# A hybrid attention layer: the order of loads, fillers and small operations ahead of its first projection

## The chip, the cores and the metric

The kernel runs on one core of a Trainium2 chip. The metric is device time in microseconds of one execution; the median of several runs counts. Five engines work side by side, each through its own queue in order: PE (matmuls; its loads of weights are shown as PEld), DVE (VectorE), ACT (ScalarE), POOL (GpSimd) and SP, which here issues DMAs only. They wait for one another and for DMAs by semaphores.

## The reference, cut to what matters

One decoder layer: a modulated norm, one projection, two groups of attention heads, an output projection with a gate. The change touches only the first two lines and the gate's factor.

```python
mod = jax.nn.silu(c) @ w_ada + b_ada
shift, scale, gate = jnp.split(mod, 3, axis=-1)
h = rms_norm(x, norm_gain) * (1 + scale[:, None, :]) + shift[:, None, :]
proj = h @ w_in
...                      # sliding-window heads, compressed/selected/window heads, z gates
out = y.astype(x.dtype) @ w_out
return x + gate[:, None, :] * out
```

x is 512 x 1024 in f32, c has 1024 values, `w_ada` is 1024 x 3072, `w_in` 1024 x 3096.

## The kernel before, in words

x is held transposed: eight tiles `xT[k]` of 128 channels x 512 tokens. Everything is f32, and most products are split in a high and a low part (`hh`, `hl` of h; `wh`, `wl` or `swh`, `swl` of a weight), so that a product is three matmuls.

Phase one makes h and the first projection (`first_proj`, L286 and L287: 768 columns into six PSUM banks) channel tile by channel tile. For a tile k it needs the root of the mean square of x for all 512 tokens (so all eight tiles of x), and the tile's shift and scale.

*The head* is all that stands ahead of tile 0. In the order of the code: SP issues x's tiles 0 to 2, the constants `first` (c in columns, `b_ada`, `norm_gain`, an identity) and `bias`, x's tiles 3 to 7, and then for four tiles the modulation weights (`ada`, two DMAs of 512 KB) and the first projection's weights (`wst`, 384 KB), then `rest`. PE runs 16 filler matmuls on zeros (`dummies`, L310). ACT squares each tile of x (L325) and DVE adds the squares of four tiles (L327); PE sums them over the channels with a column of ones (L339), after tile 3 and after tile 7. silu(c) is made in columns as c(1+tanh(c/2))/2 (L323, L329, L330). Between the last squares PE spreads it along a row with eight transposes (L333); ACT copies that row to all partitions as `scrow` (L342). PE then multiplies the bias table by its one-hot matrix (L335), and ACT copies the result (L343, L344), which two DMAs store to DRAM for the attention biases.

After L339's second group DVE makes the root (L351, then eight operations of `rsqrt`, L101 to L108). PE modulates tile 0 (`mod_pe`, L230: 8 products of 32 columns against `ada[0]`), ACT copies the result (`macc`, L233), PE sums it over partitions (`mod_col`, L250) and spreads the root with four transposes (L357), followed by three fillers. DVE finishes shift and scale (`mod_ab`, L255 and L256, columns of `AB`) and multiplies x by the root (`scaled`, L270), ACT applies shift and scale (`hh`, L365), and the first projection starts.

Tile 1 is modulated by PE in the same way, in the middle of tile 0's projection; `PE_MODS = 2` says so. For the other six tiles DVE does it with two long multiply-and-sum operations over 1024 columns each (`mod_rows`, L222), which read `scrow`. `new_tile(k)` queues, in this order, ACT's `hh` and `hf` of tile k, DVE's `mod_rows(k+1)`, `hl` of tile k (L279), `scaled(k+1)`, and the split of the next `wst` (`swh` on ACT, L262; `swl` on DVE, L265).

`in_order(tc)` around phase one keeps every engine's instructions in the order in which the code writes them. Which tiles share storage is found by the allocator, and a shared place adds waits that the code doesn't show. The later phases (other projections in a stream beside the attention slots, then the output projection) are unchanged but for `gate_slice` (L686), which reads `scrow` too.

Of the kernel before, what the change touches and what calls it, by code (L numbers as in the profile page):

```python
# [29 lines left out]
WAIT_L, WAIT_M = 4, (0, 8)  # L30
PER_A, PER_B = 3.6, (3.5, 1.6, 7)
NEAR = 256
ND = (16, 0, 3)
NR = 4
LW = 4
PE_MODS = 2
# [45 lines left out]
def hybrid_layer_kernel(ctx, tc, A, out):  # L82
# [14 lines left out]
    def rsqrt(v, n):  # L97

        y = sm.tile([128, n], F32, name="n_y")
        t = sm.tile([128, n], F32, name="n_t")  # L100
        DVE.tensor_scalar(y.bitcast(I32), v.bitcast(I32), -0.5, float(MAGIC), op0=OP.mult, op1=OP.add)  # L101
        DVE.tensor_tensor(t, y, y, op=OP.mult)
        DVE.scalar_tensor_tensor(t, t, -0.375 * NEWTON[0], v, op0=OP.mult, op1=OP.mult)
        DVE.scalar_tensor_tensor(y, t, 0.375 * NEWTON[0] * NEWTON[1], y, op0=OP.add, op1=OP.mult)
        DVE.tensor_tensor(t, y, y, op=OP.mult)
        DVE.scalar_tensor_tensor(t, t, 64.0 / 9.0, v, op0=OP.mult, op1=OP.mult)
        DVE.scalar_tensor_tensor(t, t, -10.0 / 3.0, t, op0=OP.add, op1=OP.mult)
        DVE.scalar_tensor_tensor(y, t, 5.0, y, op0=OP.add, op1=OP.mult)  # L108
        return y
# [20 lines left out]
    nsink = con.tile([128, 8], F32, name="nsink")  # L130
    sc_col = con.tile([128, 8], F32, name="sc_col")
    prm1 = con.tile([128, 8], F32, name="prm1")
    prmg = con.tile([128, 8], F32, name="prmg")
    va = con.tile([128, NB, 128], F32, name="va")
    vs = con.tile([128, NB, 128], F32, name="vs")
    vw = con.tile([128, NB, 128], F32, name="vw")
# [74 lines left out]
    def load_wst(k):  # L211
        wst[k] = wst_ring[:, k % NR]
        SP.dma_start(wst[k], A["w_qkv_a"][k])
# [4 lines left out]

    def mod_rows(k):

        for e, (factor, start) in enumerate(((1.0, prm[:, k:k + 1]), (prm[:, 24 + k:25 + k], prmg[:, k:k + 1]))):
            DVE.tensor_tensor_reduce(out=ada[k][:, e], in0=ada[k][:, e], in1=scrow, scale=factor, scalar=start,  # L222
                                     op0=OP.mult, op1=OP.add, accum_out=AB[:, k, 1 - e:2 - e])

# [39 lines left out]
    def weights_low(k):  # L264
        DVE.tensor_tensor(ws[k][1], wst[k], ws[k][0].bitcast(F32), op=OP.subtract)  # L265
# [24 lines left out]
    with in_order(tc) as begun:  # L290
        zero = con.tile([128, 512], BF16, name="zero")
        DVE.memset(zero, 0.0)
        DVE.memset(ada_ring[:, 0, 0:1], 0.0)
        DVE.memset(wst_ring[:, 0, 0:1], 0.0)
        POOL.memset(lsb[0:8, 0:LINE - NEAR], BIG)
        for k in range(8):
            SP.dma_start(xT[k], A["xT"][k])
            if k == 2:
                SP.dma_start(first, A["first"])
                SP.dma_start(bl, A["bias"])  # L300
        for k in range(NR):
            load_ada(k)
            load_wst(k)
        SP.dma_start(rest, A["rest"])
        DVE.memset(scz, 0.0)


        def dummies(n):
            for _ in range(n):
                PE.matmul(pj_kv[0].rearrange("p a b -> p (a b)"), zero[:, 0:128], zero, start=True, stop=True)  # L310

        dummies(ND[0])

        halves = [slice(0, 256), slice(256, 512)]
        pr = ps_pj.tile([128, 512], F32, name="pj")
        pl = pj_q[1][0:40, 0:NEAR]
        th = con.tile([128, 8], F32, name="th")
        for k in range(8):
            sq = stp.tile([128, S], F32, name="sacc") if k == 4 else T2(F32, "sq")
            if k % 4 == 0:  # L320
                sacc = sq
            if k == 4:
                ACT.activation(th, cT, AF.Tanh, scale=0.5)  # L323
            for c in (halves if k == 7 else [slice(0, S)]):
                ACT.activation(sq[:, c], xT[k][:, c], AF.Square)  # L325
                if k % 4:
                    DVE.tensor_tensor(sacc[:, c], sacc[:, c], sq[:, c], op=OP.add)  # L327
            if k == 4:
                DVE.scalar_tensor_tensor(sc_col, th, 1.0, cT, op0=OP.add, op1=OP.mult)  # L329
                DVE.tensor_scalar(sc_col, sc_col, 0.5, None, op0=OP.mult)  # L330
            if k == 7:
                for j in range(8):
                    PE.transpose(pj_q[2 + j // 4][:, 128 * (j % 4):128 * (j % 4) + 128],  # L333
                                 sc_col[:, j:j + 1].to_broadcast([128, 128]), ident)
                PE.matmul(pl, bl[:, NEAR:NEAR + 40], bl[:, 0:NEAR], start=True, stop=True)  # L335
                dummies(ND[1])
            if k % 4 == 3:
                for tb in range(NB):
                    PE.matmul(pr[:, tb:tb + 1], sacc[:, tb * 128:(tb + 1) * 128], ones, start=k == 3 and tb == 0,  # L339
                              stop=k == 7 and tb == NB - 1, skip_group_check=True)  # L340
        for e in range(2):
            ACT.activation(scrow[:, 512 * e:512 * e + 512], pj_q[2 + e], AF.Copy)  # L342
        ACT.copy(lsb[0:40, LINE - NEAR:LINE], pl)  # L343
        ACT.copy(lsb[32:40, 0:LINE - NEAR], lsb[32:40, LINE - NEAR:LINE - NEAR + 1].to_broadcast([8, LINE - NEAR]))  # L344
        for a in range(2):
            SP.dma_start(line_d[a], lsb[32 * a:32 * a + 8, :])
        DVE.tensor_copy(scz[:, :, 0], sc_col)
        DVE.tensor_scalar(prm1, prm[:, 8:16], 1.0, None, op0=OP.add)
        DVE.tensor_tensor(prmg, prm1, prm[:, 24:32], op=OP.mult)
        sx = con.tile([128, NB], F32, name="sx")  # L350
        DVE.tensor_scalar(sx, pr[:, 0:NB], 1.0 / D, EPS, op0=OP.mult, op1=OP.add)  # L351
        rx = rsqrt(sx, NB)
        mod_pe(0)
        mod_col(0)
        rbp = ps_pj.tile([128, 512], F32, name="pj")
        for tb in range(NB):
            PE.transpose(rbp[:, tb * 128:(tb + 1) * 128], rx[:, tb:tb + 1].to_broadcast([128, 128]), ident)  # L357
        dummies(ND[2])
        weights_high(0)
        mod_ab(0)  # L360
        scaled(0, rbp, halves)
        rb = stp.tile([128, S], F32, name="rb")
        hf[0] = T2(F32, "hf")
        for c in halves:
            ACT.activation(hh[0][:, c], y[0][:, c], AF.Identity, bias=AB[:, 0, 1:2], scale=AB[:, 0, 0:1])  # L365
        ACT.activation(rb, rbp, AF.Copy)
        ACT.activation(hf[0], y[0], AF.Identity, bias=AB[:, 0, 1:2], scale=AB[:, 0, 0:1])
        weights_low(0)
        scaled(1, rb)
        h_low(0)  # L370
        weights_high(1)
        weights_low(1)

        def new_tile(k):

            h_high(k, halves if k < 4 else (slice(0, S),))
            if k < 7:
                mod_rows(k + 1)
            h_low(k)
            if k < 7:  # L380
                scaled(k + 1, rb)
                weights_high(k + 1)
                weights_low(k + 1)

        for k in range(8):
            if k + NR < 8:
                load_ada(k + NR)
                load_wst(k + NR)
            elif k == LW:
                for _ in range(5):  # L390
                    load_next()
            for n in range(3):
                first_proj(k, n)
                if k == 0 and n == 0:
                    mod_pe(1)
                if k < 7 and n == 1:
                    if k == 0:
                        mod_col(1)
                        mod_ab(1)
                    new_tile(k + 1)  # L400
                if k >= 6 and n == 1:
                    split_to("kv_cmp", 2 * (k - 6) + 1, 0)
        DVE.tensor_tensor(kg[:, 0], qga, kga, op=OP.mult)
        DVE.tensor_tensor(kg[:, 1], qgb, kgs, op=OP.mult)
        DVE.tensor_tensor(kg[:, 2], qgb, kgw, op=OP.mult)
        DVE.tensor_tensor(kg[:, 3], qgb, kgc, op=OP.mult)
        DVE.tensor_scalar(kg[:, 0:3], kg[:, 0:3], -(HD ** -0.5), None, op0=OP.mult)
        DVE.tensor_scalar(kg[:, 3], kg[:, 3], HD ** -0.5, None, op0=OP.mult)
        DVE.tensor_scalar(nsink, sinks, -1.0, None, op0=OP.mult)
# [272 lines left out]
    def gate_slice(q):  # L682

        for h in range(2):
            n, w = 2 * q + h, raws[f"gate{q}", h]
            DVE.tensor_tensor_reduce(out=w, in0=w, in1=scrow, scale=1.0, scalar=prm[:, 16 + n:17 + n],  # L686
                                     op0=OP.mult, op1=OP.add, accum_out=gate[:, n:n + 1])
            load_next()
            yield 0.0
# [327 lines left out]
def _layout(inp):  # L1017
# [47 lines left out]
    for n in range(2):  # L1065
        bias[0:32, NEAR + 32 * n:NEAR + 32 * n + 8] = g("rel_bias")[:, 8 * n:8 * n + 8]
        bias[32, NEAR + 32 * n:NEAR + 32 * n + 8] = 1.0
    a["bias"] = bias
    return a


# [14 lines left out]
```

## Time and profile before

| what | value |
|---|---|
| runs of the kernel | 320.7, 320.85 (median), 322.26 us |
| profiled execution, whole time | 322.89 us |
| profiled execution, span | 321.1 us |
| PE busy | 310.7 us (97% of the span) |
| DVE busy | 236.4 us (74%) |
| ACT busy | 196.2 us (61%) |
| mean granted clock of PE | 0.978 |

Times in views are microseconds from the start of the span. A line of the timeline has start, length, engine, source line, operation, the tile written and the tiles read, shape, count, and in brackets the idle time before it with what ended it. A line of the windows has a stretch, its length, busy time and count of each engine, the granted share of PE's clock, the DMA share and GB/s. The column of the clock shows 1.00 before its first recorded change, at 6.85 us; the first sixteen fillers start 0.43 us apart up to there, and matmuls of the same 512 columns later in the run 0.23 us apart.

### The profile page before, as it was taken

What the parts mean: (1) busy time and instruction counts of PE and PEld (TensorE: products, weight loads), DVE (VectorE), ACT (ScalarE), POOL (GpSimd) and SP (SyncE); (2) the same over time, 40 slices, a digit from 0 to 9 for tenths busy, and PEclk for the clock granted to TensorE, in tenths of its full rate; (3) what the DMA queues carried; (4) which work ended last, traced back from release to release, by engine and by line L of the source; (5) the groups of instructions that cost most, each with busy time, mean ns of one, the idle gap of its engine ahead of it and who ended that gap; (6) DMA issues with size and microseconds to landing.
All of it is one profiled execution on the core that took longest, in us unless ns stands there. A gap on an engine that the chain in (4) does not pass through costs nothing.

```text
span 321.1 us, 5773 instructions
## 1 busy us (share of the span) xinstructions
PE 310.7 (97%) x2093; PEld 254.2 (79%) x2094; DVE 236.4 (74%) x655; ACT 196.2 (61%) x472; POOL 3.8 (1%) x21
## 2 busy tenths in 40 slices
PE   7899999999999999999999999999999999999995
PEld 2658878879888899999875788878788878788883
DVE  2548999999996467898998899989776678544220
ACT  4646556948886667495946766878785877513000
POOL 0000000000000000000000000000000000000000
PEclk9659999999999999999999999999999999999999
DMA  6999946910084535461263202322320210153201
GB/s 223 387 408 407 395 144 182 331 42 0 9 276 146 174 123 154 143 219 45 61 233 134 66 2 67 131 65 68 114 83 2 67 65 3 63 168 95 101 33 65
DMA packets 27943, 44.11 MB, mean 137 GB/s; under 512 B 1755, under 2 KB 19324, under 8 KB 27916
## 3 DMA queue, kind: packets, MB, share of 16 engines
q1 hardware_dynamic: 26764, 41.66, 37.8%
q10 hardware_dynamic: 1152, 2.10, 2.2%
q8 instruction: 16, 0.26, 0.3%
q14 instruction: 11, 0.09, 0.1%
HBM read 41.61 MB, written 2.14 MB: 136 GB/s over the span
## 4 chain that ended last, share of the span: by engine, by line
PE 61%; DVE 24%; DMA 6%; ACT 4%; issue 3%; SPq 1%; DVEq 0%; ACTq 0%
PE pj L465 25%; PE po L926 7%; PE s L851 7%; PE pj L455 4%; PE pt L909 4%; DVE wl L174 4%; DMA raw<-in_w_gate 3%; DVE ada_ring L222 3%; PE pt L899 3%; PE s L584 2%; DVE qs L516 2%; DMA xTp<-in_xT 1%; DMA ada_ring<-in_w_ada_rows 1%; DVE pa L856 1%; PE po L932 1%
## 5 line engine op out<-in xcount | busy, mean ns | idle before, releaser
L173 ACT ACTIVATE wh<-raw 128x512 fp32r<-128x512 f32 (+1 forms) x52 | 31.2, 634 | 13.5 <-PE pj L465 13.3
L174 DVE TENSOR_TENSOR wl<-raw,wh 128x512 fp32r<-128x512 f32 (+1 forms) x52 | 34.6, 690 | 5.4 <-ACT wh L173 3.4
L455 PE MATMUL pj<-wl,hh 128*128 128x256 f32 (+1 forms) x128 | 36.8, 288 | 0.2
L455 PE MATMUL pj<-wh,hh 128*128 128x256 f32 (+1 forms) x128 | 36.8, 288 | 0.0
L455 PE MATMUL pj<-wh,hl 128*128 128x256 f32 (+1 forms) x128 | 36.4, 284 | 0.0
L863 ACT ACTIVATE pp<-pp,nm 128x256 f32<-128x256 f32 (+2 forms) x48 | 29.3, 613 | 6.8 <-DVE nm L856 6.6
L465 PE MATMUL pj<-hh,wh 128*128 128x512 f32 x80 | 32.2, 402 | 0.0
L465 PE MATMUL pj<-hh,wl 128*128 128x512 f32 x80 | 31.9, 398 | 0.0
L465 PE MATMUL pj<-hl,wh 128*128 128x512 f32 x80 | 31.8, 398 | 0.0
L856 DVE CUSTOM_DVE_ANT_0 pp<-s,bias 128x256 f32<-128x256 f32 (+2 forms) x48 | 25.5, 552 | 3.7 <-PE s L851 3.5
L465 PE MATMUL pj<-yl,wh 128*128 128x512 f32 x64 | 25.2, 397 | 0.0
L465 PE MATMUL pj<-yh,wh 128*128 128x512 f32 x64 | 25.2, 397 | 0.0
L465 PE MATMUL pj<-yh,wl 128*128 128x512 f32 x64 | 25.0, 394 | 0.0
L1013 DVE SCALAR_TENSOR_TENSOR fin<-pj,gate,xr 128x512 f32<-128x512 f32 x8 | 6.0, 751 | 25.4 <-PE pj L465 25.4
L455 PEld LDWEIGHTS pj<-wl,hh 128*128 128x128 f32 x128 | 24.1, 188 | 0.7 <-DVE wl L174 0.7
L455 PEld LDWEIGHTS pj<-wh,hh 128*128 128x128 f32 x128 | 24.0, 188 | 0.3 <-issue 0.2
L455 PEld LDWEIGHTS pj<-wh,hl 128*128 128x128 f32 x128 | 24.1, 189 | 0.2 <-issue 0.2
L851 PE MATMUL s<-kTb,qs 128*128 128x256 f32 (+2 forms) x96 | 23.5, 356 | 0.0
L884 DVE TENSOR_SCALAR pp<-pp,rr,grev 128x256 f32<-128x256 f32 (+2 forms) x48 | 21.1, 477 | 0.7
L910 ACT COPY ptT<-pt 128x384 f32<-128x384 f32 (+1 forms) x32 | 15.8, 531 | 7.2 <-PE pt L909 6.8
L900 ACT COPY ptT<-pt 128x512 f32<-128x512 f32 (+1 forms) x28 | 15.5, 553 | 6.7 <-PE pt L899 6.5
L465 PEld LDWEIGHTS pj<-hh,wh 128*128 128x128 f32 x80 | 15.0, 188 | 3.8 <-issue 1.2
(233 smaller groups left out, 710.7 us busy)
## 6 DMA issues: line engine op xcount, KB each, us to landing
ada_ring<-in_w_ada_rows SPq DMA_DIRECT2D x12, 512.0 KB, 8.1
raw<-in_w_cmp SPq DMA_DIRECT2D x8, 512.0 KB, 7.7
raw<-in_w_gate SPq DMA_DIRECT2D x8, 512.0 KB, 5.3
raw<-in_w_o SPq DMA_DIRECT2D x8, 512.0 KB, 3.8
wst_ring<-in_w_qkv_a SPq DMA_DIRECT2D x8, 384.0 KB, 7.8
xTp<-in_xT SPq DMA_DIRECT2D x8, 256.0 KB, 4.7
ada_ring<-in_w_ada_cols SPq DMA_DIRECT2D x4, 512.0 KB, 7.9
bias<-line_d SPq DMA_DIRECT2D x8, 256.0 KB, 3.1
```

Of the source, the lines that this page charges most:

```text
L173: ACT.activation(wh, src, AF.Copy)
L174: DVE.tensor_tensor(wl, src, wh.bitcast(F32), op=OP.subtract)
L455: PE.matmul(bank[:, t * n:(t + 1) * n], h[:, tb * 128:(tb + 1) * 128], w[:, k % 2, :], start=k == 0 and m == 0, stop=k == 7 and m == 2)
L465: PE.matmul(bank, w, h, start=k == 0 and m == 0, stop=k == 7 and m == 2)
L851: PE.matmul(ps, qs[h][:, 128 * i:128 * i + 128], k[:, hl_, lo:lo + w], start=hl_ == 0, stop=hl_ == 1)
L856: DVE.tensor_tensor_reduce(out=P[:, g, 0:w], in0=ps, in1=bt, scale=1.0, scalar=init, op0=OP.add, op1=OP.min, accum_out=nm[:, g:g + 1])
L863: ACT.activation(P[:, g, 0:e], P[:, g, 0:e], AF.Exp, bias=nm[:, g:g + 1], scale=-1.0, accum_out=dn[:, g:g + 1])
L884: DVE.tensor_scalar(v, v, rr[:, g:g + 1], gates[:, g, br:br + 1], op0=OP.mult, op1=OP.mult)
L900: ACT.copy(T[:, :, 0:nb, :], rev(pt[:, 0:2 * nb * 128].rearrange("p (g b q) -> p g b q", g=2, b=nb)))
L909: PE.transpose(pt[:, b * 128:(b + 1) * 128], P[:, g, b * 128:(b + 1) * 128], ident)
L910: ACT.copy(T[:, 0:nb, :], rev(pt[:, 0:nb * 128].rearrange("p (b q) -> p b q", b=nb)))
L926: PE.matmul(o[64 * g:64 * g + 64, 128 * i:128 * i + 128], vb[:, 64 * g:64 * g + 64], sl["T"][g][:, b, :], start=first_of and b == 0, stop= ...
```

## The change

Seven edits, all in the head or for its sake.

- x's eight tiles are issued in one row; `first` and `bias` follow them.
- `scrow` is no longer made by transposes. A DMA behind `ada[0]` and `wst[0]` loads c, broadcast to 128 partitions (512 KB written from one row of 4 KB). After tile 0's operations ACT takes tanh of the row in two halves and DVE multiplies, so that `scrow` holds c(1+tanh(c/2)), twice silu; the factor 0.5 goes into `mod_rows` and `gate_slice`.
- silu(c) in columns is made after the loop over x's tiles, and written directly to `scz`.
- The root comes ahead of the three small products of the parameters.
- The bias product follows L339's second group, while DVE makes the root.
- The root's transposes come ahead of `mod_col(0)`, and `scaled(0)` is cut around `mod_ab(0)`.
- Fillers: 20 at the start, 4 after L339's first group, 2 after the bias product, 2 after the root's transposes, 3 after `mod_col(0)`.

```diff
-ND = (16, 0, 3)
+ND = (20, 2, 2, 3, 4)
...
-        for e, (factor, start) in enumerate(((1.0, prm[:, k:k + 1]), (prm[:, 24 + k:25 + k], prmg[:, k:k + 1]))):
+        for e, (factor, start) in enumerate(((0.5, prm[:, k:k + 1]), (prmg[:, 8 + k:9 + k], prmg[:, k:k + 1]))):
...
         for k in range(8):
             SP.dma_start(xT[k], A["xT"][k])
-            if k == 2:
-                SP.dma_start(first, A["first"])
-                SP.dma_start(bl, A["bias"])
+        SP.dma_start(first, A["first"])
+        SP.dma_start(bl, A["bias"])
         for k in range(NR):
             load_ada(k)
             load_wst(k)
+            if k == 0:
+                src = A["c"]
+                SP.dma_start(scrow, bass.AP(tensor=src.tensor, offset=src.offset, ap=[[0, 128], [1, D]]))
...
-            if k == 4:
-                ACT.activation(th, cT, AF.Tanh, scale=0.5)
...
-            if k == 4:
-                DVE.scalar_tensor_tensor(sc_col, th, 1.0, cT, op0=OP.add, op1=OP.mult)
-                DVE.tensor_scalar(sc_col, sc_col, 0.5, None, op0=OP.mult)
-            if k == 7:
-                for j in range(8):
-                    PE.transpose(pj_q[2 + j // 4][:, 128 * (j % 4):128 * (j % 4) + 128],
-                                 sc_col[:, j:j + 1].to_broadcast([128, 128]), ident)
-                PE.matmul(pl, bl[:, NEAR:NEAR + 40], bl[:, 0:NEAR], start=True, stop=True)
-                dummies(ND[1])
             if k % 4 == 3:
...
+            if k == 3:
+                dummies(ND[4])
-        for e in range(2):
-            ACT.activation(scrow[:, 512 * e:512 * e + 512], pj_q[2 + e], AF.Copy)
+        ACT.activation(th, cT, AF.Tanh, scale=0.5)
+        DVE.scalar_tensor_tensor(sc_col, th, 1.0, cT, op0=OP.add, op1=OP.mult)
+        DVE.tensor_scalar(scz[:, :, 0], sc_col, 0.5, None, op0=OP.mult)
+        sx = con.tile([128, NB], F32, name="sx")
+        DVE.tensor_scalar(sx, pr[:, 0:NB], 1.0 / D, EPS, op0=OP.mult, op1=OP.add)
+        rx = rsqrt(sx, NB)
+        DVE.tensor_scalar(prm1, prm[:, 8:16], 1.0, None, op0=OP.add)
+        DVE.tensor_tensor(prmg[:, 0:8], prm1, prm[:, 24:32], op=OP.mult)
+        DVE.tensor_scalar(prmg[:, 8:16], prm[:, 24:32], 0.5, None, op0=OP.mult)
+        PE.matmul(pl, bl[:, NEAR:NEAR + 40], bl[:, 0:NEAR], start=True, stop=True)
+        dummies(ND[1])
         ACT.copy(lsb[0:40, LINE - NEAR:LINE], pl)
...
         mod_pe(0)
-        mod_col(0)
         rbp = ps_pj.tile([128, 512], F32, name="pj")
...
         dummies(ND[2])
+        mod_col(0)
+        dummies(ND[3])
         weights_high(0)
+        scaled(0, rbp, halves[:1])
         mod_ab(0)
-        scaled(0, rbp, halves)
+        scaled(0, rbp, halves[1:])
...
         weights_low(1)
+        throw = T2(F32, "throw"), T2(F32, "throw")
+        for e in range(2):
+            ACT.activation(throw[e], scrow[:, 512 * e:512 * e + 512], AF.Tanh, scale=0.5)
+        for e in range(2):
+            v = scrow[:, 512 * e:512 * e + 512]
+            DVE.scalar_tensor_tensor(v, throw[e], 1.0, v, op0=OP.add, op1=OP.mult)
```

More of the change, by code (lines that the diff above doesn't have):

```diff
@@ L132, in hybrid_layer_kernel @@
     prm1 = con.tile([128, 8], F32, name="prm1")
-    prmg = con.tile([128, 8], F32, name="prmg")
+    prmg = con.tile([128, 16], F32, name="prmg")
     va = con.tile([128, NB, 128], F32, name="va")
@@ L346, in hybrid_layer_kernel @@
             SP.dma_start(line_d[a], lsb[32 * a:32 * a + 8, :])
[L347 to L352, printed above, removed]
         mod_pe(0)
-        mod_col(0)
         rbp = ps_pj.tile([128, 512], F32, name="pj")
@@ L685, in gate_slice @@
             n, w = 2 * q + h, raws[f"gate{q}", h]
-            DVE.tensor_tensor_reduce(out=w, in0=w, in1=scrow, scale=1.0, scalar=prm[:, 16 + n:17 + n],
+            DVE.tensor_tensor_reduce(out=w, in0=w, in1=scrow, scale=0.5, scalar=prm[:, 16 + n:17 + n],
                                      op0=OP.mult, op1=OP.add, accum_out=gate[:, n:n + 1])
@@ L1068, in _layout @@
     a["bias"] = bias
+    a["c"] = cc(g("c").reshape(1, D))
     return a
```

## The prediction

> **What bounds the kernel now.** I read the page first, then the 3.41 us windows of the engines, then the chain that ended last over the first 60 us, then the timeline, the waits and the DMA view of that stretch.
>
> ```profile
> span 321.1 us, 5773 instructions
> ```
>
> ```profile
> 3.43:6.85 3.42, 3.42 (x10) 1.22 (x9) 1.39 (x2) 1.86 (x3) 0.00 (x0) 1.00 0.98 297
> 6.85:10.26 3.41, 1.80 (x13) 1.19 (x12) 1.43 (x4) 2.42 (x5) 0.00 (x0) 1.00 0.94 312
> 10.26:13.67 3.41, 3.41 (x15) 2.29 (x13) 1.98 (x7) 2.66 (x7) 0.00 (x0) 0.50 1.00 391
> 13.67:17.08 3.41, 2.97 (x22) 1.61 (x21) 1.47 (x9) 0.63 (x2) 0.00 (x0) 0.50 1.03 417
> 17.08:20.50 3.42, 3.14 (x11) 2.25 (x13) 1.63 (x5) 1.75 (x4) 0.00 (x0) 0.50 1.03 408
> 20.50:23.91 3.41, 3.41 (x16) 2.29 (x20) 1.66 (x3) 1.39 (x3) 0.00 (x0) 0.50 1.02 406
> ...
> 26.74:58.53 31.79, 31.79 (x177) 26.69 (x175) 31.01 (x53) 19.83 (x33) 0.00 (x0) 1.00 0.76 270
> 58.53:321.10 262.57, 255.68 (x1815) 213.71 (x1813) 194.02 (x567) 163.28 (x418) 3.20 (x16) 1.00 0.31 100
> ```
>
> The columns are stretch, length, busy time (and count) of PE, PEld, DVE, ACT and POOL, granted clock, DMA share, GB/s. After 58.53 PE is busy for 255.68 of 262.57 us; from 26.74 to 58.53 DVE is busy for 31.01 of 31.79. So from 26.74 on the work is dense, and what moves its start moves the end. The change touches only the head ahead of 26.74. There the clock is half from 10.26 to 23.91, exactly four stretches of 3.41 us. It fell after the stretch in which PE was busy for 1.80 of 3.41, and came back only after one filled by long matmuls. Stretches filled for 2.97 to 3.41 us by transposes, one-column products and loads of weights didn't bring it back.
>
> ```profile
> 9.22 1.05 PE pj L339 x8
> 10.28 1.70 PE sq L333 x8
> 11.98 1.00 PE sq L335 x2
> 12.98 1.80 PE pj L339 x8
> 14.78 1.91 PE pj L230 x16
> ...
> 17.14 1.01 PE pj L250 x4
> 18.16 0.95 PE pj L357 x4
> ...
> 20.39 0.66 PE sq L286
> ...
> 24.55 0.43 PE sq L286
> ...
> 26.16 0.35 PE pj L250 x4
> ...
> 26.54 0.16 DVE AB L255
> ...
> 26.82 1.20 DVE ada_ring L222
> ```
>
> This is the chain (start, length). From 9.22 to 20.39 it is PE's own queue: sums of squares (L339), the eight transposes that spread silu(c) (L333), the bias product (L335), the second sums, tile 0's modulation (L230, L250), the root's transposes (L357). L339 takes 1.05 at full clock and 1.80 at half.
>
> **The change, part by part.** The x loads first.
>
> ```profile
> 1.23 6.39 PE L310 MATMUL skv<-zero 128*128 128x512 bf16 x16 [1.23 <-DVE wst_ring L294]
> ...
> 3.07 2.25 SPq L297 DMA_DIRECT2D xTp<-in_xT  x5
> ...
> 7.81 0.98 SPq L205 DMA_DIRECT2D ada_ring<-in_w_ada_cols  x2
> ...
> 9.10 0.33 SPq L213 DMA_DIRECT2D wst_ring<-in_w_qkv_a  x1
> ...
> 14.82 0.16 DVE L351 TENSOR_SCALAR sx<-pj 128x4 f32<-128x4 f32 x1 [2.33 <-PE pj L339]
> ...
> 16.40 0.16 DVE L108 SCALAR_TENSOR_TENSOR n_y<-n_t,n_y 128x4 f32<-128x4 f32 x1
> ...
> 24.63 0.85 ACT L262 ACTIVATE swh<-wst_ring 128x768 fp32r<-128x768 f32 x1 [2.75 <-PE pj L230]
> ...
> 25.38 0.37 ACT L233 ACTIVATE macc<-pj 128x256 f32<-128x256 f32 x1
> ```
>
> ```profile
> L325 ACT ACTIVATE sq<-xTp x8: 400/630/632, 3.6 to 10.7; 128x512 f32<-128x512 f32 x6, 128x256 f32<-128x256 f32 x2
> L270 DVE TENSOR_TENSOR xTp<-xTp,pj x2: 414/418/422, 19.2 to 19.5; 128x256 f32<-128x256 f32 x2
> ...
> L365 ACT ACTIVATE hh<-xTp,AB x2: 585/592/600, 19.6 to 20.1; 128x256 fp32r<-128x256 f32 x2
> ...
> DMA to landing us min/median/max: 3.0/4.7/5.5
> ```
>
> The last of x's five late issues starts at 3.07+4x0.45=4.87 and lands by 4.87+5.5=10.37. `first` and `bias` (84 and 38 KB) now queue behind it; at the 391 to 417 GB/s of the windows that is 0.3 us, so x ends at 10.07. Bounds: nothing gained, or, if the small loads are also what held tile 3 back, some 1.7 us (five tiles of 256 KB at 0.65 us after 5.0). I take 0.3, which is bytes alone.
>
> Tile 7's squares come in halves of 0.40, then an add of a half (0.42 for that shape, L270): the sums are ready at 11.2, and L339 follows directly, because the transposes (1.70) and the bias product (1.00) no longer stand before it. It began at 12.98; now it runs from 10.85 (first half) to 11.9 at full clock. Then follow the bias product (half of 1.00) to 12.4 and two fillers at 0.21 (sixteen took 6.39, 0.43 each while cold) to 12.85.
>
> ```profile
> ada_ring<-in_w_ada_cols SPq DMA_DIRECT2D x1, 512.0 KB, 7.8
> ...
> ada_ring<-in_w_ada_cols SPq DMA_DIRECT2D x1, 512.0 KB, 8.7
> ...
> DMA to landing us min/median/max: 6.5/7.8/9.3
> ...
> bias<-line_d SPq DMA_DIRECT2D x8, 256.0 KB, 3.1
> ```
>
> Tile 0's modulation now meets its load: the second half of `ada` 0, issued about 5.8, lands 7.8 later at 13.6, with the same bytes ahead of it as before. Eight of the sixteen records run before that, eight after (half of 0.95): 14.1. The root is the row pair 14.82 to 16.56, 1.74 us, so 11.95 to 13.7, hidden by the same load; its transposes (half of 0.95) end at 14.6. Two fillers: 15.0; L250 (half of 1.01): 15.5. AB takes 26.54 to 26.82, 0.28; `hh`'s first half 0.59: 16.5 with the handovers. The first projection began at 20.39; that is **3.8 us earlier**. It is the ends that fall: 2.7 of transposes and bias product ahead of the root, and the half clock on all the rest.
>
> The first projection's first third takes 1.5 at full clock (24.55 to 26.16 with the start): 18.0. The broadcast load of c adds 512 KB to the queue ahead of `ada` 1; by bytes 1.27 us at 412 GB/s. All 128 of its rows read one 4 KB row. The nearest case are the overlapping bias windows, 256 KB in 3.1 us, against 3.0 for the fastest x tile of that size: no penalty seen. Bounds 1.27 to double. `ada` 1's second half landed at 8.46+8.7=17.2, now 18.45; T, the end of tile 1's modulation, is then 18.95 (was 24.6).
>
> ```profile
> ACT swh L262 <- PE pj L230: 2.7, 1, 2.7
> ...
> L771 ACT ACTIVATE zth<-pj x8: 572/580/606, 177.0 to 257.9; 128x512 f32<-128x512 f32 x8
> L773 DVE SCALAR_TENSOR_TENSOR sza<-zth,pj x4: 679/680/689, 177.7 to 205.8; 128x512 f32<-128x512 f32 x4
> ```
>
> Here the change adds work to the path. ACT's `swh` 1 waited 2.7 us for L230's end, though it reads no result of it, so it probably shares storage with something that L230 reads; I keep that wait. Behind it ACT now has two tanh of 128x512 (0.63, the longest such row) before it copies `macc` 1, and PE's L250 waits for that copy. `wst` 1, issued at 9.10, lands within 9.3, plus 1.27: 19.7 at the latest; I take 19.5. Then `swh` to 20.25 (25.38-24.63), tanh to 21.5, `macc` 21.9, L250 22.3, AB 22.6. On DVE `swl` 1 (0.95) and the two products of 0.68 end at 22.65 as well. So mod_rows(2) starts at **22.8 against 26.74: 3.9 us**. From T it is 3.9 us instead of 2.1: the moved silu gives back 1.2 in ACT order, and the DMA 0.6.
>
> Costed at nothing: the small tanh of c with its two column products (0.2 each, done by 11.5 while PE has L339; beyond 11.9 they would delay the root one for one); the three products of `prm` (0.17 each, between 13.7 and 14.2, under L230 and L357); the copies of the bias line (ACT, 12.4 to 13.3, under the wait for `ada` 0); the twenty first fillers (thirteen at 0.43 up to 6.85, seven at half of that, end 8.3; L339's first group can't start before, and ends at 9.35, hidden by x, which is needed until 10.9); four fillers behind that group (to 10.2, before 10.85); three behind L250, 0.64 at full clock, under AB and `hh` (1.0), but at half clock 1.3, which is 0.3 too long; the factors 0.5, which change constants alone. SP issues one DMA more, 0.33 of its queue as in the L213 row, while the transfers ahead are still landing (7.8 us each), and no store passes it; POOL's queue is untouched. Gone from the path are the two copies to `scrow` on ACT.
>
> Sum against the profiled execution: 321.1-3.9=317.2 of span; it took 322.89 in all, so 319.0. That execution is 2.04 above the median of the runs, 320.85 (320.7 to 322.26). I can't see how much of the 2.04 is recording and how much a later return of the clock; if it were all clock, the median run has 1.9 left to gain. I take 3.2 for the median: **317.6**. Bounds of the clock case: 315.5 (x without its 1.7 us, mod_rows(2) at 21.4, gain 5.3) to 319.0.
>
> [...]
>
> **The rivals.**
>
> *B, the clock closes again in the middle.* In 10.26 to 13.67 PE would be busy for 2.4 of 3.41 us, most of it one-column work. The 1.80 that closed it is below that, the filled stretches that stayed open above. If it closes at 13.67, L230's rest ends at 14.6, L357 15.55, two fillers 16.4, L250 17.4, first projection 18.7. The next stretch is dense but for L250; reopened at 20.5, T is 22.0 and mod_rows(2) 25.3 (1.4 gained); reopened at 23.9, T is 23.4 and it starts at 26.7, as before. With 0.7 off as above: 320.2 to 321.6, about 320.4.
>
> *C, slower: the clock falls at 10.26 as before*, because the four fillers don't count for enough. Then L339 runs 10.85 to 12.75, bias 13.75, fillers 14.6, L230 16.5, L357 17.5, fillers 18.3, L250 19.35, AB and `hh` 20.65, the projection's third 2.8, T 24.9; the tanh pair sits behind it and mod_rows(2) starts at 28.2: 1.5 later, with 0.7 as above 2.2, 323.0. The point is the granted clock at 10.3; for it speaks the half clock in the rows above, against it that PE has 3.3 of the 3.41 us filled, 2.3 of them by fillers.
>
> *D, the broadcast load is slow or the change only trades waits:* at double price it takes 1.27 more, `ada` 1 and `wst` 1 are later by that: 318.9. Against it stands the 3.1 us row.
>
> **How the numbers follow.** Forecast (clock held) 0.48, D 0.11, B 0.28, C 0.13. Half a per cent, about what a measurement tells from no change, is 1.6 us: below 319.25 lie the forecast, 0.08 of D and 0.03 of B, 0.59. Within: 0.03 of D, 0.24 of B, 0.27. Above 322.45: C and 0.01 of B, 0.14. The range 315.5 to 321.4 leaves out C and a tail of B and of early x. The forecast alone would be 315.5 to 319.0.
>
> **What would show it.** Granted clock full from about 6.9 on without a half-rate stretch; L339's second group ending near 11.9; L230 split by the wait for `ada` 0 near 13.6; the first projection near 16.5; `macc` 1 behind two tanh at 21.5; mod_rows(2) at 22.8; the 4.5 us beat of DVE unchanged after it. Wrong would be a half clock at 14 (B) or 11 (C), a c load that lands over 1.5 us behind `wst` 0 (D), `swh` 1 free of L230, or a later stage that gives the head start back.

## The result, and the profile after

| | before | after |
|---|---|---|
| median of 7 runs | 321.15 us | 318.09 us |
| fastest to slowest | 320.7 to 322.26 | 317.5 to 319.58 |
| ratio after / before, 95% interval | | 0.9899 [0.9876, 0.9922] |
| profiled execution, whole time | 322.89 us | 317.5 us |
| its span, mean granted clock | 321.1 us, 0.978 | 315.7 us, 0.998 |

The kernel became 1.0% faster. The edit moves the line numbers: the sums of squares are now L330, the bias product L343, the root's transposes L352, `hh` of tile 0 L363, the tanh of c's row L373, its products L376. In the windows of the engines of the changed kernel, the head is cut as it was for before; the last two rows are the dense part of phase one, from `mod_rows(2)` on, and all that follows:

```profile
3.43:6.85 3.42, 3.42 (x10) 1.22 (x9) 1.34 (x2) 2.45 (x4) 0.00 (x0) 1.00 0.89 296
6.85:10.26 3.41, 3.35 (x20) 1.83 (x18) 2.12 (x4) 2.69 (x6) 0.00 (x0) 1.00 1.04 324
10.26:13.67 3.41, 2.90 (x28) 1.65 (x28) 2.55 (x14) 0.88 (x2) 0.00 (x0) 1.00 1.01 401
13.67:17.08 3.41, 3.02 (x24) 2.03 (x18) 2.17 (x8) 2.68 (x5) 0.00 (x0) 1.00 1.02 416
17.08:20.50 3.42, 3.42 (x30) 2.14 (x28) 2.23 (x3) 2.54 (x5) 0.00 (x0) 1.00 1.03 416
20.50:23.91 3.41, 2.96 (x19) 2.64 (x19) 3.41 (x8) 2.23 (x6) 0.00 (x0) 1.00 1.03 405
21.93:53.81 31.88, 31.84 (x177) 26.74 (x176) 31.10 (x54) 19.96 (x33) 0.00 (x0) 1.00 0.88 324
53.81:315.70 261.89, 255.57 (x1814) 213.58 (x1812) 193.68 (x567) 162.84 (x417) 3.30 (x16) 1.00 0.31 103
```

The column of the granted clock is 1.00 in every stretch; before it was 0.50 in four of them. The stretch 6.85 to 10.26, in which PE was busy for 1.80 us, now has 3.35. Of the two long rows the first is as long as before (31.88 against 31.79 us) and the second 0.68 us shorter (261.89 against 262.57). So most of the time came out of the head, and nothing gave it back. The steps of the head are in the timeline of the changed kernel (start, length, engine, line, operation, in brackets the idle time before and its end):

```profile
8.36 0.95 PE L330 MATMUL pj<-ones,sq 128*128 128x1 f32 x8
9.17 1.02 PE L312 MATMUL skv<-zero 128*128 128x512 bf16 x4
10.77 1.05 PE L330 MATMUL pj<-ones,sacc 128*128 128x1 f32 x8 [0.58 <-DVE sacc L327]
11.75 0.62 PE L343 MATMUL sq<-raw 33*40 33x256 f32 x2
...
12.31 0.60 PE L312 MATMUL skv<-zero 128*128 128x512 bf16 x2
...
12.84 1.07 PE L230 MATMUL pj<-ada_ring,scz 128*32 128x256 f32 x16
13.85 0.65 PE L352 MATMUL pj<-first,n_y 128*128 128x128 f32 x4
...
16.28 0.51 PE L286 MATMUL sq<-swh,hh 128*128 128x512 f32 x1 [0.34 <-ACT hh L363]
...
17.87 1.07 PE L230 MATMUL pj<-ada_ring,scz 128*32 128x256 f32 x16
18.78 0.85 ACT L262 ACTIVATE swh<-wst_ring 128x768 fp32r<-128x768 f32 x1 [0.88 <-DMA wst_ring<-in_w_qkv_a]
19.53 1.13 ACT L373 ACTIVATE throw<-scrow 128x512 f32<-128x512 f32 x2
20.54 1.28 DVE L376 SCALAR_TENSOR_TENSOR scrow<-throw,scrow 128x512 f32<-128x512 f32 x2
20.57 0.36 ACT L233 ACTIVATE macc<-pj 128x256 f32<-128x256 f32 x1
21.93 1.28 DVE L222 CUSTOM_DVE_ANT_0 ada_ring<-ada_ring,scrow,first 128x1024 f32<-128x1024 f32 x1
```

The first projection starts at 16.28 (before: 20.26 in the same view) and `mod_rows(2)` at 21.93 (before: 26.74). What is late now is another thing, as the chain that ended last in the first 60 us shows (start, length, what):

```profile
4.01 5.36 DMA xTp<-in_xT
9.39 0.33 SPq L205
9.76 8.99 DMA wst_ring<-in_w_qkv_a
18.78 0.24 ACT swh L262
...
19.53 1.13 ACT throw L373 x2
20.67 0.28 ACT macc L233
20.99 0.61 PE pj L250 x4
```

PE's own queue, which carried the chain of before from 9.22 to 20.39, is gone from it. The chain is x's last tile (landed at 9.37), the issues on SP behind it, then the transfer of `wst` 1 (landed at 18.75), then ACT's queue: split, tanh pair, copy of tile 1's sums.

One profile is not the whole result. The seven executions of the changed kernel fall into groups by their mean granted clock: 317.5 and 317.54 us at 0.998, 317.79 to 318.4 at 0.994 and 0.995 (four), 319.58 at 0.989. One stretch of 3.41 us at half clock, in 318, is 0.005. So the clock held throughout in two executions, was half for one stretch in four, and for two stretches in one. The kernel before, run beside each of the three groups of experiments below, was at 0.976 to 0.989 in all of 77 executions (two to some four such stretches), with 319.15 to 319.9 us in nearly all those at 0.987 to 0.989, 320.3 to 321.5 at 0.981 to 0.984, 321.8 to 323.3 below. This is the key to the experiments: each was run 6 to 12 times, and beside the median stands how many of its executions had a clock of 0.997 or more ("held"). The ratio is estimated over all executions but two slow ones (e8's 323.47 and e10's 323.33 us), and need not be the quotient of the medians.

| kernel | order | fillers (start, after first sums, after bias product, after root, before `hh`) | median us | ratio, 95% interval | held |
|---|---|---|---|---|---|
| before (three groups) | old | 16, 0, 0, 3, 0 | 320.62, 320.82, 320.65 | | 0 of 77 |
| after | new | 20, 4, 2, 2, 3 | 318.09 | 0.9899 [0.9876, 0.9922] | 2 of 7 |
| e1 | new | 16, 0, 0, 3, 0 | 318.63 | 0.9939 [0.991, 0.9968] | 0 of 12 |
| e2 | old | 20, 4, 2, 3, 0 | 317.74 | 0.9909 [0.9876, 0.9942] | 6 of 6 |
| e9 | old | 20, 0, 0, 3, 0 | 320.44 | 1.0001 [0.9978, 1.0025] | 0 of 12 |
| e10 | old | 16, 4, 0, 3, 0 | 318.46 | 0.9953 [0.9918, 0.9988] | 6 of 12 |
| e3 | new, tanh first | 20, 4, 2, 2, 3 | 318.69 | 0.9932 [0.9902, 0.9961] | 3 of 12 |
| e4 | new, c later | 20, 4, 2, 2, 3 | 318.3 | 0.9928 [0.9896, 0.9959] | 1 of 12 |
| e5 | new, constants early | 20, 4, 2, 2, 3 | 319.31 | 0.9954 [0.9927, 0.9981] | 1 of 12 |
| e8 | new, row by transposes | 20, 4, 2, 2, 3 | 319.75 | 0.9983 [0.9944, 1.0021] | 6 of 12 |
| e6 | new | 20, 6, 3, 3, 5 | 317.63 | 0.9902 [0.9865, 0.9938] | 6 of 7 |
| e7 | new, tanh first, c later | 20, 6, 3, 3, 5 | 317.32 | 0.9899 [0.9865, 0.9934] | 7 of 7 |
| e11 | new, tanh first | 20, 6, 3, 3, 5 | 317.45 | 0.9906 [0.9877, 0.9935] | 6 of 6 |
| e12 | new, c later | 20, 6, 3, 3, 5 | 316.78 | 0.9885 [0.9856, 0.9915] | 6 of 6 |

### The profile page after: what moved, and what is told of

It reads as the page before. It is cut to its first block, busy times and chain, and to the rows that moved or that the text cites. A ratio compares the mean times of both kernels' runs of the same rounds, so it can differ in the third digit from the quotient of the medians.

```text
span 315.7 us, 5779 instructions
## 1 busy us (share of the span) xinstructions
PE 306.7 (97%) x2097; PEld 250.9 (79%) x2098; DVE 237.2 (75%) x657; ACT 195.8 (62%) x472; POOL 3.9 (1%) x21
## 4 chain that ended last, share of the span: by engine, by line
PE 76%; DVE 10%; DMA 6%; ACT 4%; issue 2%; SPq 1%; POOL 0%; ACTq 0%; DVEq 0%; POOLq 0%
PE pj L469 29%; PE pj L459 9%; PE po L930 7%; PE s L855 7%; PE sq L286 7%; PE pt L913 4%; PE skv L287 3%; PE pt L903 3%; DMA wst_ring<-in_w_qkv_a 3%; PE s L588 3%; DVE qs L520 2%; DMA xTp<-in_xT 2%; DMA raw<-in_w_gate 2%; DVE kTb L538 1%; DVE wl L174 1%
## 5 line engine op out<-in xcount | busy, mean ns | idle before, releaser
L469 PE MATMUL pj<-yh,wl 128*128 128x512 f32 x64 | 25.1, 394 | 0.0
```

Of the source, the lines that this page charges most:

```text
L469: PE.matmul(bank, w, h, start=k == 0 and m == 0, stop=k == 7 and m == 2)
```

## The experiments

**Order or fillers? e1 and e2** cut the change in two.

```diff
 e1, on the changed kernel
-ND = (20, 2, 2, 3, 4)
+ND = (16, 0, 3, 0, 0)
 e2, on the kernel before
-ND = (16, 0, 3)
+ND = (20, 2, 3, 0, 4)
...
+            if k == 3:
+                dummies(ND[4])
```

> The changed kernel with 16 fillers at the start, three behind the root's transposes and none elsewhere, as many as before. Theory (the full clock in the head is held by the added fillers): the granted clock falls at the end of a 3.41 us stretch between 10 and 14 us and comes back between 20 and 24; mod_rows(2), at 21.93 in the changed kernel, starts at 24 to 27; time 0.994 to 1.003 of before. Rival (the order of the work alone gives the gain: with the transposes gone nothing needs fillers): the clock stays full, mod_rows(2) starts at 21.5 to 22.0 and the time is 0.990 of before.

> The kernel before with fillers alone added: 20 at the start, 4 behind the first group of sums, 2 behind the bias product, three behind the root's transposes as before. Theory (clock): the clock stays full from 6.9 us on, all of PE's head halves, mod_rows(2) starts near 23 instead of 26.7 and the time is 0.990 to 0.994 of before. Rival (order): transposes keep it from holding or the fillers only lengthen PE's queue; mod_rows(2) at 26 to 28, time 0.998 to 1.004.

The fillers alone give about all of the gain: 0.9909 against 0.9899, and the clock held in all six executions. The new order alone gives 0.9939, but it too works mostly through the clock: its executions lie at 0.995 to 0.984 (317.2 to 317.8, 318.6 to 319.3, 319.7 to 320.6 us), one or two stretches better than before, some 1.2 to 1.4 us a stretch. Its profile is one of the worst of the twelve: the clock fell at 11.63 and came back at 21.87, and `mod_rows(2)` started at 24.9, as the theory had it. At equal clock little of the order's gain is left: at 0.987 to 0.989 e1 has 318.6 to 319.3 where before has mostly 319.2 to 319.9, some 0.6 us; with the clock held, the old order (e2: 317.49 to 318.51; e10 below: 317.31 to 317.9) and the new (317.5, 317.54) can't be told apart. The timeline of e2 shows why:

```profile
9.97 1.04 PE L333 MATMUL sq<-first,sc_col 128*128 128x128 f32 x8
10.93 0.62 PE L335 MATMUL sq<-raw 33*40 33x256 f32 x2
...
11.93 0.95 PE L339 MATMUL pj<-ones,sacc 128*128 128x1 f32 x8
12.81 1.07 PE L230 MATMUL pj<-ada_ring,scz 128*32 128x256 f32 x16
...
16.63 0.50 PE L286 MATMUL sq<-swh,hh 128*128 128x512 f32 x1 [0.50 <-ACT hh L367]
...
19.36 0.85 ACT L262 ACTIVATE swh<-wst_ring 128x768 fp32r<-128x768 f32 x1 [1.11 <-PE pj L230]
20.12 0.36 ACT L233 ACTIVATE macc<-pj 128x256 f32<-128x256 f32 x1
...
21.49 1.28 DVE L222 CUSTOM_DVE_ANT_0 ada_ring<-ada_ring,scrow,first 128x1024 f32<-128x1024 f32 x1
```

At full clock the transposes and the bias product cost 1.04 and 0.62 us, and tile 0's modulation starts no later for them: 12.81 against 12.84. With them PE is busy while x's last tiles are squared; the changed kernel idles there for 0.58 us, and has the bias product and two fillers between the second sums and the modulation instead (its rows at 11.75 and 12.31). The first projection starts only 0.35 later than in the changed kernel, and `mod_rows(2)` 0.44 earlier, for ACT copies tile 1's sums at 20.12 with no tanh pair ahead of it, against 20.57. What follows the first projection took 0.58 us longer in e2 than in the changed kernel (262.75 against 262.17; e8 below shows why), so equal times don't mean that each part is equal.

**Which fillers? e9 and e10** put one group alone into the kernel before.

```diff
 e9
-ND = (16, 0, 3)
+ND = (20, 0, 3)
 e10: as e2, with
+ND = (16, 0, 3, 0, 4)
```

> The kernel before with twenty instead of sixteen fillers at the start, nothing else. Theory (several holes have to be filled, because the 3.41 us stretches in which the clock is decided lie elsewhere in each execution; fillers alone, at the start, behind the first sums and behind the bias product, held the clock in six of six): the start fillers alone end at about 8.5 instead of 7.6 and leave the work from 9.2 on as thin as it was, so the clock still closes in most executions: mean clock 0.984 to 0.995, median 319.0 to 320.4. Rival (the hole from 7.6 to 9.2 us alone closed the gate): clock 0.997 or more in nearly all executions, median 317.4 to 318.2.

> The kernel before with four fillers behind the first group of sums of squares, nothing else. Theory (several holes count): the hole from 7.6 to 9.2 stays, the clock closes in most executions, mean clock 0.982 to 0.995, median 319.0 to 320.6; the fillers may delay the transposes by up to 0.85 us in executions that are at full clock there. Rival (dense work behind 9.2 us is what holds it): clock 0.997 or more in nearly all executions, median 317.4 to 318.2.

The rival of e9 fell: with the hole of before (7.6 to 9.2 us) filled, nothing is gained. The windows of e9:

```profile
6.85:10.26 3.41, 3.41 (x25) 2.37 (x23) 2.49 (x6) 3.33 (x8) 0.00 (x0) 1.00 1.05 317
10.26:13.67 3.41, 2.74 (x27) 1.45 (x26) 2.54 (x15) 1.61 (x4) 0.00 (x0) 1.00 1.01 390
13.67:17.08 3.41, 2.91 (x15) 2.00 (x11) 1.01 (x6) 1.47 (x3) 0.00 (x0) 0.54 1.02 417
17.08:20.50 3.42, 3.42 (x14) 2.28 (x16) 2.31 (x4) 2.04 (x4) 0.00 (x0) 0.50 1.03 411
```

The clock no longer falls at 10.26; it falls one stretch later, behind 2.74 us of one-column sums, transposes and the wait for `ada` 0 (0.55 us in its timeline). All twelve executions lost two or three stretches (0.982 to 0.989). This is rival B of the prediction at work, in the old order. e10 was better than its theory and worse than its rival: six executions held (317.31 to 317.9), six lost one to some four stretches (319.0 to 323.33). So the four behind the first sums do more than the four at the start, and in the old order only the groups together (e2) held the clock every time. In the new order the same 20, 4 and 2 fillers held it in two of seven: with the transposes gone, PE has other holes (0.58 us ahead of the second sums).

**x's order. e5** issues `first` and `bias` behind x's third tile again.

```diff
             SP.dma_start(xT[k], A["xT"][k])
-        SP.dma_start(first, A["first"])
-        SP.dma_start(bl, A["bias"])
+            if k == 2:
+                SP.dma_start(first, A["first"])
+                SP.dma_start(bl, A["bias"])
```

> The changed kernel with one part undone: `first` and `bias` are issued behind x's third tile again. Theory (x's order is worth what the last tile of x lands earlier: 9.38 us in the changed kernel against 10.37 before): the last tile of x lands 0.6 to 1.0 us later, the second group of sums of squares starts at 11.4 to 11.8 instead of 10.77, and the first projection follows it by the same, 16.9 to 17.3 instead of 16.28; executions without a half-clock stretch take 318.1 to 318.5, the median 318.4 to 319.2. Rival (bytes alone, 0.3 us, as the prediction had it, or ada 0's second half sets the start of the projection anyway): the projection starts within 0.3 us of 16.28 and the median is within 0.4 of 318.1.

In the chain and in the timeline of e5 x's last tile lands at 4.89+6.08=10.97, its squares wait for it until 10.99, and the second sums start at 11.91, 1.14 later than in the changed kernel:

```profile
4.89 6.08 DMA xTp<-in_xT
```

```profile
10.99 0.72 ACT L326 ACTIVATE sq<-xTp 128x256 f32<-128x256 f32 x2 [0.52 <-DMA xTp<-in_xT]
...
11.91 1.87 PE L331 MATMUL pj<-ones,sacc 128*128 128x1 f32 x8 [0.68 <-DVE sacc L328]
```

In these two profiles x's order moves its last tile by 1.6 us (10.97 against 9.37) and the sums by 1.14, not by 0.3. In time, at one lost stretch (0.994, 0.995) e5 has 318.83 to 319.09 and the changed kernel 317.79 to 318.4: some 0.8 us. But the one execution of e5 that held the clock took 317.58, as little as the changed kernel's 317.5 and not the 318.1 to 318.5 expected, so what the order is worth with the clock held stays open. The rest of its 1.2 us in the median is again clock: six of twelve executions lost two stretches. In the profile PE idles for 1.77 us ahead of the first sums, where the changed kernel has no gap. The start of the projection (20.46) can't be set against the 16.9 to 17.3 expected, as this profile has two half-clock stretches from 11.76 on.

**silu(c)'s row. e3** takes tanh and products ahead of the split of tile 1's weights, **e4** issues the load of c behind tile 1's weights, **e8** goes back to the transposes, behind the second sums.

```diff
 e3
-        weights_high(1)
-        weights_low(1)
         throw = T2(F32, "throw"), T2(F32, "throw")
...
             DVE.scalar_tensor_tensor(v, throw[e], 1.0, v, op0=OP.add, op1=OP.mult)
+        weights_high(1)
+        weights_low(1)
 e4
-            if k == 0:
+            if k == 1:
                 src = A["c"]
 e8
-            if k == 0:
-                src = A["c"]
...
+        for j in range(8):
+            PE.transpose(pj_q[2 + j // 4][:, 128 * (j % 4):128 * (j % 4) + 128],
+                         sc_col[:, j:j + 1].to_broadcast([128, 128]), ident)
+        for e in range(2):
+            ACT.activation(scrow[:, 512 * e:512 * e + 512], pj_q[2 + e], AF.Copy)
...
+        mod_pe(0)
         ACT.copy(lsb[0:40, LINE - NEAR:LINE], pl)
...
-        mod_pe(0)
...
-        throw = T2(F32, "throw"), T2(F32, "throw")
...
```

In e8 the block of `throw` goes with the load, the factors are 1.0 again, and the copies of the bias line come behind tile 0's modulation.

> The changed kernel with the two tanh of c's row and their products queued ahead of the split of tile 1's weights instead of behind it. Theory (the pair stands in ACT's and DVE's order ahead of tile 1's macc while ACT is idle 0.88 us for wst 1): tanh from 17.9, swh 1 near 19.05, macc 1 near 19.85 instead of 20.57, mod_rows(2) near 21.2 instead of 21.93; time 0.7 us or 0.2% below the changed kernel. Rival (the load of wst 1 sets it, the pair is hidden): mod_rows(2) within 0.2 of 21.9, same time.

> The changed kernel with c's broadcast load issued behind wst 1 instead of behind wst 0. Theory (its 512 KB delay ada 1 and wst 1 by about 1.2 us, and swh 1 waits for wst 1): wst 1 lands near 17.6 instead of 18.76, swh 1 starts near 17.9 right behind hf, tanh when c lands near 18.8, macc 1 near 20.0, mod_rows(2) near 21.2 to 21.4; 0.5 to 0.7 us below the changed kernel. Rival (load order makes no difference, or the late c is now the last wait): mod_rows(2) at 21.9 or later.

> The changed kernel with one part undone: silu(c)'s row is made by eight transposes again, now behind the second sums of squares, where PE waits for the root and for ada 0's second half; no load of c, no tanh of the row, no products behind it. Theory (the broadcast load costs the queue 1.2 us and the tanh pair 1.3 us of ACT ahead of tile 1's copy, and the transposes are hidden by the wait for ada 0): ada 1 lands 1.2 us earlier, tile 2's modulation on DVE starts at 20.0 to 20.8 instead of 21.93, and executions at full clock take 315.8 to 316.6. Rival (the transposes stand on PE's path: tile 0's modulation starts at 13.7 instead of 12.84, the projection at 17.1, and DVE's start is set by it): mod of tile 2 at 21.5 to 22.0, median 317.4 to 318.2.

By their medians e3 and e4 look like nothing or worse, but their executions split by clock: where it held, e3 took 316.53 to 316.78 (three of twelve) and e4 316.01 (one), 0.7 to 1.0 and 1.5 us below the changed kernel's 317.5; where one stretch was lost, 318.34 to 319.35 and 317.66 to 318.68, no better than the changed kernel's 317.79 to 318.4. Both profiles lost one stretch, so their starts of `mod_rows(2)`, 23.12 and 22.92, say nothing against the 21.2 expected. Four executions are thin evidence for a shorter path; e11 and e12 below repeat it with the clock held.

e8 is a miss: with the clock held (six of twelve) it took 318.57 to 319.25, over 1 us more than the changed kernel, where 315.8 to 316.6 was expected. Its head with the clock held isn't known: the profile lost two stretches, and `mod_rows(2)` started at 25.1. But some 1.1 us of the excess show behind the head. From the last matmul of the first projection to the end of the span the profile of e8 has 263.25 us (56.75 to 320.0), that of the changed kernel 262.17 (53.53 to 315.7). The two programs have the same later code but for the factor 0.5, yet PE's matmuls come in another order there: the order is planned anew when a kernel is built, and another head can give another one. Over the fourteen traces there are just two orders behind the first projection. One is that of the changed kernel, e1, e4 to e7 and e12, whose remainders are 261.85 to 262.33; the other is that of before, e2, e3 and e8 to e11, with 262.34 to 263.25. On average the two lie 0.7 us apart. That the order is the cause is argued from one profile of each kernel, not tried by itself, and the rest of e8's excess stays open. Since the remainder differs by up to 1.4 us, a difference of medians below about 1 us is not a measure of the head alone.

**Holding the clock. e6, e7, e11, e12** put more fillers into the holes that the changed kernel has left (10.2, 14.5 and 15.9 us), alone and with the moves of e3 and e4.

```diff
 all four, on the changed kernel
-ND = (20, 2, 2, 3, 4)
+ND = (20, 3, 3, 5, 6)
```

> The changed kernel with the filler counts (20,3,3,5,6) instead of (20,2,2,3,4), so that PE's holes at 10.2, 14.5 and 15.9 us are filled. Theory (what separates 317.5 from 318.4 and 319.6 in the changed kernel is one or two stretches of half clock, which holes of PE let in; fillers alone in the old order held the clock in all of six executions): no execution has a mean clock below 0.997, the median falls to 317.4 to 317.8, and tile 2's modulation on DVE still starts at 21.9 to 22.3. Rival (one-column products and transposes count for little whatever is between them, or the fillers themselves delay tile 0's work): half-clock stretches in a good part of the executions as before, median 318.0 to 319.0.

> All three together: the filler counts (20,3,3,5,6), tanh of the row and its products ahead of the split of tile 1's weights, the load of c behind tile 1's weights. Theory (the two moves each took about 1 us off at equal clock, 316.5 and 316.0 against 317.5, and the fillers hold the clock): median 315.8 to 316.6, executions all at clock 0.997 or more. The two moves may not add, since with c loaded later its tanh comes later than the weights of tile 1: then tanh waits for the load (landing near 20 us) and the weights' split waits behind it, median 316.6 to 317.5. Rival (the dips come whatever PE does): median 317.5 to 318.5.

> The changed kernel with the filler counts (20,3,3,5,6) and the tanh of the row with its products ahead of the split of tile 1's weights; the load of c stays behind tile 0's. Theory (at equal clock the move alone took 0.9 us off, 316.5 to 316.8 against 317.5, since ACT does the tanh while it would wait for tile 1's weights; the fillers hold the clock): clock 0.998 or more, median 316.4 to 317.1, tile 2's modulation on DVE at 21.2 to 21.7. Rival (the start of that modulation is set by other things, and the difference came from the order of the later stages, which is built anew for each kernel): median 317.2 to 318.2 with the clock held.

> The changed kernel with the filler counts (20,3,3,5,6) and c loaded behind tile 1's weights; the tanh of the row stays behind their split. Theory (at full clock the one such execution without the fillers took 316.0; ada 1 and wst 1 land 1.2 us earlier): clock 0.998 or more, median 315.8 to 316.6. Rival (as with both moves together, tanh waits for the load near 20 us and holds the copy of tile 1's sums behind it): tile 2's modulation at 22.3 to 23.0, median 317.0 to 318.0.

With these six more fillers 25 of 26 executions held the clock, against 2 of 7 and 4 of 24 of the same orders without (changed kernel; e3 and e4). So in these runs it was PE's holes that let the clock fall. Yet e6 is no better than the changed kernel by the ratio (0.9902, 0.9899), and only 0.46 us by the median: the fillers seem to have a price too. Where the clock held, e3 and e4 took some 0.5 to 0.8 us less without them (316.53 to 316.78, 316.01) than e11 and e12 with them (317.04 to 317.53, 316.49 to 316.94); that is four executions, on another chip and in other builds. Of the two moves, c's later load looks worth 0.5 us by the ratios of e12 and e6, 0.85 by their medians. The earlier tanh is worth nothing that can be told (0.9906 and 317.45 against 0.9902 and 317.63), though `mod_rows(2)` starts at 21.68 in e11's profile and at 22.27 in that of e6: e11 has the slower order behind the head, as its rival (317.2 to 318.2) feared. e3's gain at held clock is not borne out. Both together (e7) lose what e12 has, as was feared; the timelines of e7 (of its slowest execution, 318.49) and then of e12:

```profile
20.04 1.15 ACT L371 ACTIVATE throw<-scrow 128x512 f32<-128x512 f32 x2 [0.85 <-DMA scrow<-in_c]
21.10 0.83 ACT L262 ACTIVATE swh<-wst_ring 128x768 fp32r<-128x768 f32 x1
```

```profile
17.91 0.83 ACT L262 ACTIVATE swh<-wst_ring 128x768 fp32r<-128x768 f32 x1
18.64 1.14 ACT L373 ACTIVATE throw<-scrow 128x512 f32<-128x512 f32 x2
19.68 0.36 ACT L233 ACTIVATE macc<-pj 128x256 f32<-128x256 f32 x1
...
21.25 1.27 DVE L222 CUSTOM_DVE_ANT_0 ada_ring<-ada_ring,scrow,first 128x1024 f32<-128x1024 f32 x1
```

In e7 ACT waits for c, and the split, with no wait of its own, stands behind it. In e12 `wst` 1 is there when ACT comes to it (no wait in the row; 0.88 us in the changed kernel), c is there when the split is done, and `mod_rows(2)` starts at 21.25. The rival of e12 (22.3 to 23.0) fell. e12 is the best version: 316.78 us, 0.9885 of before, 0.2 us above the 315.8 to 316.6 expected. All six of its executions (316.49 to 316.94) are below the changed kernel's fastest, though they ran on other chips and the intervals of the two ratios overlap.

## Why the prediction was right

The time, 318.09 for 317.6, came out, and the likeliest case did in the profile and in two of seven executions. That the median came so close is luck in part, as the first points show.

- **The head's gain is what moves the end: right.** Nothing behind the head gave it back. `mod_rows(2)` came 4.81 us earlier where 3.9 was forecast, and the two profiled executions lie 5.39 us apart; the rest is mostly that what follows the first projection, with its matmuls in another order, took some 0.6 less, which the prediction didn't have. The medians lie 3.06 apart, for a forecast of 3.2. That agreement is three errors that nearly cancel: the profiles' gain was 1.49 larger than forecast, the profiled execution of before lay 1.74 above its median where 0.7 was taken off, and the median of the changed kernel lies 0.59 above its profiled execution, for which nothing was taken off.
- **"The clock held": right in the profile, in two of seven executions.** The prediction treated the held clock, B and C as outcomes of the kernel, of which one comes true. They are outcomes of an execution: held in two of seven, fallen for one stretch in four and for two in one. B was two or three stretches, with the clock back only at 20.5 or 23.9, at 2.6 to 4 us over the forecast; in the changed kernel two cost 2.1, and one, a case that the prediction doesn't have, 0.3 to 0.9. C's 323.0 was never seen. Its point, the granted clock at 10.3, was well placed, for PE had 3.35 of 3.41 us filled there.
- **The 2.04 us between the profiled execution and the median of before** was left open as recording or clock. It is clock: before's executions at the profile's 0.978, or 0.979, take 321.8 to 323.1, those at 0.981 to 0.984, where the median lies, 320.3 to 321.5. To take 0.7 of it off was too little.
- **x by "0.3, which is bytes alone": mis-sized.** The last tile landed at 9.37, 0.7 before the 10.07 forecast and within the stated bound of 1.7; in e5 it landed at 10.97. The second sums still began at 10.77 (forecast 10.85), because the step from there was sized short: the prediction gave tile 7 one half of squares and one half of adds, while ACT and DVE also had the tiles ahead of it to finish.
- **"Tile 0's modulation now meets its load": wrong, at little cost.** It was to be split by the wait for the second half of `ada` 0 at 13.6. Its sixteen records ran in one piece from 12.84, right behind the two fillers; the second half, issued about 6.1, landed 6.8 later. What stood on the path was PE's own queue of sums, bias product and fillers. The modulation ended at 13.91, forecast 14.1, so the sum hardly shows it.
- **The projection at 16.5 and the modulation of tile 1 at 18.95:** right. 16.28, and 17.87+1.07=18.94.
- **"I keep that wait" (`swh` 1 for L230): wrong, and without a price.** In the changed kernel `swh` 1 waits for its own DMA instead. The addresses in the two builds explain it: in before the buffer of `swh` 1 (3072 bytes of each partition, from 86912) covers that of `scz` (1024 bytes from 88960), which L230 reads; in the changed kernel they lie apart (103680 and 110016). In the prediction's sum the wait cost nothing, for L230 ended at 18.95 and `wst` 1 landed at 19.5. The term that was mis-sized is that landing: it came at 18.75, which makes most of the 0.9 by which `mod_rows(2)` beat 22.8.
- **"The moved silu gives back 1.2 in ACT order and DMA 0.6": right in kind.** ACT has 1.13 us of tanh ahead of the copy; e12 suggests that 0.5 to 0.85 us are to be had by issuing c one tile later.
- **D, a slow broadcast load: wrong.** The row of the load and its issue in the changed kernel:

```profile
scrow<-in_c SPq DMA_DIRECT2D x1, 512.0 KB, 7.2
```

```profile
8.03 0.33 SPq L305 DMA_DIRECT2D scrow<-in_c  x1
```

It landed at 8.03+7.2=15.2, as fast as the four loads of 512 KB for `ada` 0 and 1 (median 7.3 in the same view).

- **The reason given for the gain was too broad.** The prediction counted 2.7 us of transposes and bias product off the path beside the half clock. e2 keeps both on PE and has the same time within the noise: there the projection starts only 0.35 later. Most of the gain was the half clock, and the fillers alone are enough to take it away.

## What to carry to other kernels

A few short matmuls on zeros in PE's holes can be worth more than a better order of the work, if the row of the granted clock shows half clock behind thin stretches: here the fillers alone gave 0.9909 (e2), the order alone 0.9939 (e1). Try fillers in every hole up to the first dense stage: the changed kernel with its holes, and e3 and e4 with theirs, held the clock in 2 of 7 and 4 of 24 executions, the four kernels with six more fillers in 25 of 26. Then group the executions by their mean granted clock before medians are compared: an edit that shortens the path by 1 us can look like nothing beside half-clock stretches, which cost 1.2 to 1.4 us each in e1. Compare the order of the later instructions too: it differed between kernels whose edits lie far ahead of them, and the two orders seen lie 0.7 us apart on average. And read from the build which buffers share storage before a wait is carried over into a forecast.

## What the hardware showed that was not expected

In the heads of the seven profiles that have a fall the clock changed only at whole steps of 3.41 us from its first rise (before: rise at 6.85, fall at 10.26, rise at 23.91; e1: 4.80, 11.63, 21.87). In all fourteen that first rise lay anywhere from 4.28 (e11) to 7.22 us (e6) after the span's start, though all the kernels begin with the same sixteen fillers. That an execution meets the steps wherever they happen to lie is an estimate from these, one profile of each kernel; that the executions of one kernel fall into groups by their clock (the changed kernel at 0.998, 0.994 to 0.995 and 0.989) fits it. PE's busy time alone didn't decide whether the clock stayed. In the windows cut on each profile's own steps, of e1, e2 and e3 in turn:

```profile
4.80:8.22 3.42, 1.88 (x10) 0.67 (x7) 2.08 (x3) 2.19 (x5) 0.00 (x0) 1.00 0.97 353
8.22:11.63 3.41, 1.87 (x16) 1.78 (x16) 2.40 (x6) 1.87 (x5) 0.00 (x0) 1.00 1.04 366
```

```profile
13.65:17.06 3.41, 2.35 (x19) 1.51 (x14) 2.66 (x11) 2.31 (x5) 0.00 (x0) 1.00 1.02 416
```

```profile
9.99:13.40 3.41, 2.81 (x19) 1.43 (x21) 2.54 (x12) 1.24 (x5) 0.00 (x0) 1.00 0.97 349
```

The clock fell behind 1.87 and 2.81 us of work, and stayed behind 1.88 and 2.35. In the heads of the fourteen profiles the seven falls came behind stretches, each on its profile's own steps, with 1.80 (before), 1.87 (e1), 1.94 (e5), 2.15 (e8), 2.42 (e4), 2.68 (e9) and 2.81 us (e3) of PE work; none came behind those with 1.88 (e1), 2.35 (e2), 2.55 and 2.63 (e10), 2.60 (e5) and 2.63 us (e11). What decided in these stays open. None of the seven falls had an idle gap between PE's matmuls longer than 1.77 us (e5) ahead of it, and that of e9 none longer than 0.55, where before has 1.61.
